# Two hybrid blocks on one core: building the state space operands a group later and into the down projection, with the modulation steps shifted the same way

## The chip, the core and the metric

The kernel runs on one core of a Trainium2 chip. Time is device microseconds of one execution of the whole program, from inputs in HBM to the output in HBM. The engines are TensorE (PE in the profile; PEld is its weight load), VectorE (DVE), ScalarE (ACT), GpSimd (POOL) and SyncE (SP), whose queue issues the DMAs. Each engine works through its own queue in order.

## What is computed

256 tokens of width 1024 go through a first block of two layers (a gated delta rule beside a short convolution, then a SwiGLU network) and a second block of two layers. The part that the change touches, cut to its core:

```python
def swiglu(h, w_in, w_out):                       # w_in 1024 x 5632, w_out 2816 x 1024
    gate, up = jnp.split(h @ w_in, 2, axis=-1)
    return (jax.nn.silu(gate) * up) @ w_out

def second_block(x, c, mod_w, mod_b, ...):
    for l in range(DEPTH):                        # DEPTH = 2
        mod = (jax.nn.silu(c) @ mod_w[l] + mod_b[l]).reshape(bsz, 3, 3, D_MODEL)
        ...
        x = post_add(x, swiglu(pre(x, 0), ffn_w_in[l, 0], ffn_w_out[l, 0]), 0, FFN_RES)
        y = token_mixer(pre(x, 1), ..., ssm_a_re[l], ssm_a_im[l], ssm_log_dt[l], ssm_b_re[l], ...)
        x = post_add(x, y, 1, 1.0)
        x = post_add(x, swiglu(pre(x, 2), ffn_w_in[l, 1], ffn_w_out[l, 1]), 2, FFN_RES)
    return x
```

Inside the token mixer `s5_ssm` runs a diagonal complex state space over the tokens. Its operands, products of B and C with powers of the decay, depend on weights alone. The modulation `mod` depends on the vector `c` alone. Both can be computed at any time before they are needed, beside other work.

## The kernel before

**Matmuls.** Every large product runs in float32 by three matmuls: weights and activations are split into a high part (`wh`, `xh`, `ah`) and a rest (`wl`, `xl`, `al`), and `group` (L270 on) adds wh·xh, wh·xl and wl·xh into PSUM. A matmul has a 128x128 stationary tile of weights and 256 tokens moving. Weights come as a stream of 586 blocks of up to eight tiles (512 KB), in the order in which they are used. `prepare` (L231) loads one block through SP, makes `wh` on ScalarE (L246; in the first block often on VectorE, L244) and `wl` on VectorE (L253, a "split" below). It runs four blocks ahead; there are four buffers of raw weights and four of `wl`. One block of eight tiles is 24 matmuls.

**The networks.** `ffn` (L429) goes over 22 tiles of the hidden width in six groups of four tiles (the last has two): `gp`, the gate product (4 blocks), Silu on ScalarE (L444), `up`, the up product (4 blocks), then on VectorE the product of the two (L459) and its split into `ah` and `al` (L387, L388). The PSUM banks (`pg`, four) that the next group's gate needs come free by that product. The first group differs, since the norm of its input isn't known yet: its input is settled behind it (L147 to L154), and its products take more operations (L446, L463, L464). Then comes the down projection, eight columns of 22 tiles (24 blocks); `done` takes each column on (its square is summed on VectorE at L601). The second block has four such networks, two a layer, with weights `f2i` (gate and up) and `f2o` (down).

**Work that rides along.** A modulation step (`mod_step`, L514) loads 512 KB through SP into `mraw`, a single buffer (`MB = 1`), and multiplies and sums it on VectorE (L521). There are 144. `mod_pace` (L524) adds a rate per weight block, `MOD_RATE`, by the kind of block (`phase_of`: 0 and 1 the first block's mixer and network, 2 the second block's mixer, 3 its networks), and issues a step at each full one. The state space operands of a layer are built by `ssm_params` (L1131), a generator in 27 steps: first 512-wide products on VectorE (L1143, L1161), then transposes and copies (L1191 on TensorE, L1192 on ScalarE), then 256 small matmuls and their copies (L1204, L1210), last the tables of cosines and sines, 36 short operations on VectorE. `ssm_start` (L1120) begins it behind a group of the last network ahead of that mixer, so in the first network of the second block for its layer 0, and in the second network of that layer for layer 1. `ssm_steps(rest)` (L1125) does as many steps as an even share over `rest` further calls needs.

**The order.** All this is only the order in which the program is written. `Order` (L1647 on) then plans the whole program with prices and priorities of its own and fixes for each engine the order in which its instructions are queued; data dependences and buffers bind it. A change in one place can so move instructions in all others.

Of the kernel before, what the change touches and what calls it, by code (L numbers as in the profile page):

```python
# [17 lines left out]
KD = 8  # L18
NF = 22
# [7 lines left out]
DEPTH = 2  # L27
HI_SHARE = (0.55,0.05,0,0)
WARM = 5
MOD_RATE = (0.08,0.5,0.03,0.4)  # L30
MB = 1
FF = 2816
NSTREAM = 74973184
# [39 lines left out]
def tiles4(o):  # L73
    return [o + c * P for c in range(4)]


def all_blocks():
# [14 lines left out]
    for l in range(DEPTH):  # L92
        w, o = ("win", l), 4 * DN_WIDTH + 8
        g(w, tiles4(512), KD)
        for c in (0, 1024, 1536, o + 512, o + 1024, o):
            g(w, tiles4(c), KD)
        for c in range(KD):
            g(("wout", l), [c * P], KD)
        ffn(("fg", l), ("fu", l), ("fd", l), 0)
# [58 lines left out]
class Kern:  # L158
# [270 lines left out]
    def ffn(s, wg, wu, wd, h, done, wg0=0, wu0=0, last=False, then=None):  # L429
        nc, tc = s.nc, s.tc  # L430
        rho = h.rho
        with tc.tile_pool(name=s.nm("ffn"), bufs=1, reuse_waits="tile") as pool:
            ah = s.t(pool, [P, NF, T], "ah", F32R)
            al = s.t(pool, [P, NF, T], "al", F32R)
            for g0 in range(0, NF, 4):
                n = min(4, NF - g0)
                gp = s.group(wg, [wg0 + (g0 + c) * P for c in range(n)], KD, h.h, h.l, fresh=h.due)
                due = h.behind(then)
                s.ssm_steps(2 * ((NF - 1 - g0) // 4) + 1)
                sg = []  # L440
                for c in range(n):
                    a = s.t(pool, [P, T], "sg", bufs=4)
                    if not due:
                        nc.scalar.activation(out=a, in_=gp[c][:, :T], func=AF.Silu)  # L444
                    else:
                        nc.vector.tensor_tensor(out=a, in0=gp[c][:, :T], in1=rho, op=ALU.mult)  # L446
                        bias = {}
                        if h.shift is not None:
                            cc = s.t(pool, [P, 1], "cc", bufs=4)
                            s.shifted(cc, gp[c])  # L450
                            bias = {"bias": cc}
                        nc.scalar.activation(out=a, in_=a, func=AF.Silu, **bias)
                    sg.append(a)
                up = s.group(wu, [wu0 + (g0 + c) * P for c in range(n)], KD, h.h, h.l, fresh=h.due)
                due = h.behind(then)
                for c in range(n):
                    a = s.t(pool, [P, T], "act", bufs=2)
                    if not due:
                        nc.vector.tensor_tensor(out=a, in0=up[c][:, :T], in1=sg[c], op=ALU.mult)  # L459
                    else:  # L460
                        cc = s.t(pool, [P, 1], "cc", bufs=4)
                        s.shifted(cc, up[c])
                        nc.vector.tensor_tensor(out=a, in0=up[c][:, :T], in1=rho, op=ALU.mult)  # L463
                        nc.vector.scalar_tensor_tensor(out=a, in0=a, scalar=cc, in1=sg[c], op0=ALU.add, op1=ALU.mult)  # L464
                    s.split(ah[:, g0 + c, :], al[:, g0 + c, :], a)
                if s.later and g0 == 0:
                    s.later(pool, ah[:, 0, 0:1])
                    s.later = None
                s.ssm_steps(2 * ((NF - 1 - g0) // 4))
            s.preload(AF.Sqrt, al[0:1, NF - 1, 0:1])  # L470
            AH, AL = (lambda k: ah[:, k, :]), (lambda k: al[:, k, :])
            if last:
                for half in range(2):
                    for c, ps in enumerate(s.group_by_token(wd, tiles4(half * 512), NF, AH, AL)):
                        done(half, c, ps)
            else:
                for c in range(KD):
                    done(c, s.group(wd, [c * P], NF, AH, AL)[0][:, :T])


    def open1(s, ctx):
# [4 lines left out]
    def layer1(s, l, x):  # L486
        nc = s.nc
        h = s.pre(x, s.cols(("g1", l)))
        x = s.mixer1(l, x, h)
        h = s.pre(x, s.cols(("g2", l)))  # L490
        if l == 0:
            s.later = s.first_coefs
        if l == DEPTH - 1:
            s.first_weights(h.rho[:, 0:KD])
        s.ffn(("fg", l), ("fu", l), ("fd", l), h,
              lambda c, ps: nc.vector.tensor_tensor(out=x[:, c, :], in0=x[:, c, :], in1=ps, op=ALU.add))
        return x
# [26 lines left out]
    def mod_pace(s, spec):  # L524

        if s.sc_ is None or not s.todo:
            return
        s.credit += MOD_RATE[s.phase_of(spec)]
        while s.credit >= 1 and s.todo:
            s.credit -= 1  # L530
            s.mod_step()
# [18 lines left out]
    def layer2(s, l, z, sq, last=False, subs=(0, 1, 2)):  # L550
        for i in subs:
            if i != 1 and (l if i == 0 else l + 1) == s.next_ssm < DEPTH:
                s.later = s.ssm_start
            s.mod_done(l, i)
            gains, weights = s.modA[l][:, i * 8:i * 8 + 8], None
            if sq is None:
# [1411 lines left out]
```

## Time and profile before

| | us |
|---|---|
| median of 3 runs | 1932.19 (1929.66 to 1932.62) |
| profiled execution | 1930.54 |
| its span, first to last instruction | 1928.7 |
| TensorE busy | 1868.8 |
| VectorE busy | 1525.5 |
| ScalarE busy | 1086.4 |
| mean granted TensorE clock | 0.987 of 2.4 GHz |

Matmuls are pipelined, and a matmul's row lasts longer than its share of the engine, so a busy TensorE may still be a slow one; how many matmuls a stretch holds, and how long it takes, tells more. In the second block the first layer's first network has its gate and up products from 700.5 to 853.5 us of the span and its down projection to 915.8; the second one from 1119.0 to 1271.4 and 1333.8; the second layer's from 1338.5 to 1467.5 and 1529.8, and from 1731.0 to 1859.4 and the end.

### The profile page before, as it was taken

The page shows a single profiled execution, that of the slowest core. Times are in us where ns is not written, and L with a number is a line of the kernel's source. Part 1 is how long each engine was busy: PE and PEld are TensorE (multiplying, and loading weights), DVE is VectorE, ACT ScalarE, POOL GpSimd, SP SyncE. Part 2 cuts the span into 40 slices and gives each one's busy share as a digit, 9 for nine tenths or more (in the row PEclk, how much of TensorE's full clock was granted, in tenths as well). Part 3 has the DMA queues.
Part 4 walks back from the last instruction along what each step waited for, and adds up shares of the span by engine and source line. Part 5 has one row for each costly group of instructions (what it writes and reads, how often), then busy time and mean ns, then how long its engine had stood idle before and what let it go on. Part 6 is the DMA issues. An engine that isn't in the chain of part 4 may idle for free.

```text
span 1928.7 us, 40170 instructions
## 1 busy us (share of the span) xinstructions
PE 1868.8 (97%) x16106; PEld 1812.7 (94%) x16106; DVE 1525.5 (79%) x2908; ACT 1086.4 (56%) x2004; POOL 8.5 (0%) x20
## 2 busy tenths in 40 slices
PE   7999999899899997999999999999999999999998
PEld 7999999899899997999898988999999988999997
DVE  8979877898887889886984799887977697479553
ACT  6767644576654564454755554556554565566442
POOL 0000000000000000000000000000000000000000
PEclk8999999999999998999999998999999999999999
DMA  5424787543577775577334546676777433455553
GB/s 196 144 99 155 283 279 267 206 139 115 207 274 276 265 268 197 208 267 258 110 122 146 203 164 231 223 266 212 258 280 252 161 135 123 141 173 172 189 187 109
DMA packets 107755, 383.78 MB, mean 199 GB/s; under 512 B 11952, under 2 KB 12464, under 8 KB 107568
## 3 DMA queue, kind: packets, MB, share of 16 engines
q1 hardware_dynamic: 107280, 380.83, 56.7%
q8 instruction: 126, 2.06, 0.4%
q14 instruction: 61, 0.50, 0.1%
q10 hardware_dynamic: 288, 0.39, 0.1%
HBM read 380.12 MB, written 1.05 MB: 198 GB/s over the span
## 4 chain that ended last, share of the span: by engine, by line
PE 82%; DVE 10%; ACT 5%; issue 2%; DMA 1%; SPq 0%; DVEq 0%; ACTq 0%
PE g L286 70%; PE g L306 3%; DVE wl L253 2%; DMA wr<-in_wstream 1%; ACT wh L246 1%; PE m L1204 1%; PE m L1242 1%; DVE xs L147 1%; DVE xl L405 1%; PE m L873 1%; DVE scp L1143 1%; DVE xl L154 1%; PE m L868 1%; DVE mraw L521 1%; DVE sqa L349 1%
## 5 line engine op out<-in xcount | busy, mean ns | idle before, releaser
L286 PE MATMUL g<-xh,wh 128*128 128x256 f32 (+1 forms) x3200 | 890.1, 287 | 23.9 <-DVE act L459 7.7
L286 PE MATMUL g<-xh,wl 128*128 128x256 f32 (+1 forms) x3200 | 886.5, 286 | 5.1 <-DVE wl L253 5.0
L253 DVE TENSOR_TENSOR wl<-wr,wh 128x1024 fp32r<-128x1024 f32 (+2 forms) x586 | 696.7, 1195 | 233.1 <-PE g L286 138.7
L286 PE MATMUL g<-xl,wh 128*128 128x256 f32 x3200 | 839.9, 285 | 0.7 <-DVE xl L405 0.4
L246 ACT CAST wh<-wr 128x1024 fp32r<-128x1024 f32 (+2 forms) x538 | 553.7, 1031 | 485.3 <-PE g L286 268.0
L286 PEld LDWEIGHTS g<-xh,wh 128*128 128x128 f32 x3200 | 605.6, 191 | 33.2 <-ACT wh L246 9.6
L286 PEld LDWEIGHTS g<-xh,wl 128*128 128x128 f32 x3200 | 606.1, 191 | 8.6 <-DVE wl L253 6.6
L286 PEld LDWEIGHTS g<-xl,wh 128*128 128x128 f32 x3200 | 580.7, 191 | 2.4 <-DVE xl L154 0.9
L286 PE MATMUL g<-ah,wl 128*128 128x256 f32 x880 | 246.4, 280 | 0.0
L286 PE MATMUL g<-ah,wh 128*128 128x256 f32 x880 | 245.5, 279 | 0.0
L286 PE MATMUL g<-al,wh 128*128 128x256 f32 x880 | 245.5, 279 | 0.0
L521 DVE SCALAR_TENSOR_TENSOR mraw<-mraw,siluc 128x1024 f32<-128x1024 f32 x144 | 175.5, 1219 | 27.4 <-DMA mraw<-in_modw 27.0
L286 PEld LDWEIGHTS g<-al,wh 128*128 128x128 f32 x880 | 165.4, 188 | 0.0
L286 PEld LDWEIGHTS g<-ah,wl 128*128 128x128 f32 x880 | 165.2, 188 | 0.0
L286 PEld LDWEIGHTS g<-ah,wh 128*128 128x128 f32 x880 | 164.6, 187 | 0.0
L387 ACT CAST ah<-act 128x256 fp32r<-128x256 f32 x132 | 50.5, 405 | 74.5 <-DVE act L459 62.5
L444 ACT ACTIVATE sg<-g 128x256 f32<-128x256 f32 x108 | 40.2, 385 | 43.1 <-PE g L286 43.0
L459 DVE TENSOR_TENSOR act<-g,sg 128x256 f32<-128x256 f32 x116 | 46.3, 418 | 15.3 <-PE g L286 13.0
L388 DVE TENSOR_TENSOR al<-act,ah 128x256 fp32r<-128x256 f32 x132 | 52.2, 417 | 6.0 <-ACT ah L387 4.1
L286 PE MATMUL g<-gl,wh 128*128 128x256 f32 x128 | 36.0, 281 | 0.0
L286 PE MATMUL g<-v,wl 128*128 128x256 f32 x128 | 35.9, 281 | 0.0
L286 PE MATMUL g<-v,wh 128*128 128x256 f32 x128 | 35.8, 280 | 0.0
(467 smaller groups left out, 2189.8 us busy)
## 6 DMA issues: line engine op xcount, KB each, us to landing
wr<-in_wstream SPq DMA_DIRECT2D x538, 512.0 KB, 4.3
mraw<-in_modw SPq DMA_DIRECT2D x144, 512.0 KB, 3.9
wr<-in_wstream SPq DMA_DIRECT2D x40, 384.0 KB, 4.7
wr<-in_wstream SPq DMA_DIRECT2D x8, 256.0 KB, 5.2
stb<-in_ssmc SPq DMA_DIRECT2D x2, 512.0 KB, 3.1
sbb<-in_ssmb SPq DMA_DIRECT2D x2, 512.0 KB, 3.4
x<-in_x SPq DMA_DIRECT2D x2, 256.0 KB, 5.5
x<-in_x SPq DMA_DIRECT2D x1, 512.0 KB, 7.7
```

The source lines that it names most:

```text
L147: nc.vector.scalar_tensor_tensor(out=a, in0=s.z[:, k, :], scalar=s.gains[:, k:k + 1], in1=s.rho, op0=ALU.mult, op1=ALU.mult)
L154: nc.vector.scalar_tensor_tensor(out=s.xl[:, k, :], in0=a, scalar=s.shift[:, k:k + 1], in1=s.xh[:, k, :T], op0=ALU.add, op1=ALU.subtract)
L246: nc.scalar.copy(out=hi[:, :n], in_=raw[:, :n])
L253: e.tensor_tensor(out=lo[:, :n], in0=raw[:, :n], in1=hi[:, :n], op=ALU.subtract)
L286: nc.tensor.matmul(ps[c][:, :x.shape[-1]], wt, x, start=bi == 0 and k == 0 and i == 0, stop=bi == len(specs) - 1 and k == n - 1 and i == ( ...
L306: nc.tensor.matmul(ps[h], x(k0 + k)[:, h * P:(h + 1) * P], wt[:, k, :], start=(k0 == 0 and k == 0 and i == 0), stop=(k0 + k == kt - 1 and ...
L349: nc.vector.tensor_tensor(out=acc, in0=acc, in1=q, op=ALU.add)
L387: s.nc.scalar.copy(out=out_h, in_=src)
L388: s.nc.vector.tensor_tensor(out=out_l, in0=src, in1=out_h, op=ALU.subtract)
L444: nc.scalar.activation(out=a, in_=gp[c][:, :T], func=AF.Silu)
L459: nc.vector.tensor_tensor(out=a, in0=up[c][:, :T], in1=sg[c], op=ALU.mult)
L521: nc.vector.scalar_tensor_tensor(out=w, in0=w, scalar=1.0, in1=s.sc_, op0=ALU.mult, op1=ALU.mult, accum_out=s.mod[l][:, j:j + 1])
```

## The change

The rate of modulation steps in the second block's gate and up products falls from 0.4 to 0.3 a weight block, and in its down projections it rises to 0.6. The state space steps start behind the group at 4, the second, and no longer behind the first. Their share counts KD = 8 further calls, which are made behind each column of the down projection. `later_at` tells the two users of `later` apart: the coefficients of the first block's network still start behind the first group.

```diff
-MOD_RATE = (0.08,0.5,0.03,0.4)
+MOD_RATE = (0.08,0.5,0.03,0.3,0.6)
...
-                s.ssm_steps(2 * ((NF - 1 - g0) // 4) + 1)
+                s.ssm_steps(2 * ((NF - 1 - g0) // 4) + 1 + KD)
...
-                if s.later and g0 == 0:
+                if s.later and g0 == s.later_at:
                     s.later(pool, ah[:, 0, 0:1])
                     s.later = None
-                s.ssm_steps(2 * ((NF - 1 - g0) // 4))
+                s.ssm_steps(2 * ((NF - 1 - g0) // 4) + KD)
...
                 for c in range(KD):
                     done(c, s.group(wd, [c * P], NF, AH, AL)[0][:, :T])
+                    s.ssm_steps(KD - 1 - c)
...
-            s.later = s.first_coefs
+            s.later, s.later_at = s.first_coefs, 0
...
-        s.credit += MOD_RATE[s.phase_of(spec)]
+        s.credit += MOD_RATE[4 if spec[0][0] == "f2o" else s.phase_of(spec)]
...
-                s.later = s.ssm_start
+                s.later, s.later_at = s.ssm_start, 4
```

What the planner makes of it, at three places of the first network of the second block. First VectorE's queue ahead of the second group's products (L459). `wl` rows are splits of weights, `mraw` a modulation step, `scp`, `smi` and `stb` the state space operands, `act` the product, `r` and `x` work of the network's entry. Before:

```order
L1143 TENSOR_TENSOR scp_9613<-scp_9613,smi_9612 128x16x32
L253 TENSOR_TENSOR wl_9785<-wr_9783,wh_9784 128x1024
L1143 TENSOR_TENSOR smi_9612<-scp_9613,ssm_lam 128x512
L1143 TENSOR_TENSOR scp_9613<-scp_9613,ssm_lam 128x16x32
L1143 TENSOR_TENSOR scp_9613<-scp_9613,smi_9612 128x16x32
L253 TENSOR_TENSOR wl_9815<-wr_9813,wh_9814 128x1024
L1143 TENSOR_TENSOR smi_9612<-scp_9613,ssm_lam 128x512
L521 SCALAR_TENSOR_TENSOR mraw_9819,mod_2605<-mraw_9819,siluc 128x1024
L1143 TENSOR_TENSOR scp_9613<-scp_9613,smi_9612 128x16x32
L253 TENSOR_TENSOR wl_9848<-wr_9846,wh_9847 128x1024
L253 TENSOR_TENSOR wl_9878<-wr_9876,wh_9877 128x1024
L459 TENSOR_TENSOR act_9906<-g_9779,sg_9771 128x256
```

And now (lines behind L479 are one further on in the new file, so L522 is the modulation step and L1144 the state space operations):

```order
L632 RECIPROCAL r_9251<-sd_9219 128x256
L253 TENSOR_TENSOR wl_9750<-wr_9748,wh_9749 128x1024
L522 SCALAR_TENSOR_TENSOR mraw_9784,mod_2605<-mraw_9784,siluc 128x1024
L253 TENSOR_TENSOR wl_9780<-wr_9778,wh_9779 128x1024
L640 TENSOR_TENSOR x_76<-x_76,r_9251 128x256 x2
L1144 TENSOR_TENSOR scp_9888<-stb_9889,ssm_cr 128x16x32
L1144 TENSOR_TENSOR smi_9887<-stb_9889,ssm_ci 128x512
L459 TENSOR_TENSOR act_9871<-g_9744,sg_9736 128x256
```

Between the fourth split for the second group's gate and that product there were 21 state space operations, 3 modulation steps and 8 splits; now 2 of the first stand there. From this product to the next group's there are now 15 of them, with 8 splits and 2 modulation steps.

Second, TensorE's small matmuls of the build (`m` from `scp` and `sbb`). Before they stand among gate and up products (`xh`, `xl`):

```order
L286 MATMUL g_10567<-xh_9172,wh_10492 128x256
L286 MATMUL g_10567<-xl_9173,wh_10492 128x256
L286 MATMUL g_10567<-xh_9172,wl_10493 128x256
L1204 MATMUL m_10694<-scp_9613,sbb_9615 32x32
L1204 MATMUL m_10694<-scp_9613,sbb_9615 32x128
L1204 MATMUL m_10694<-scp_9613,sbb_9615 32x96
L1204 MATMUL m_10694<-scp_9613,sbb_9615 32x64
```

Now they stand among the matmuls of the down projection (`ah`, `al`):

```order
L1205 MATMUL m_11074<-scp_9888,sbb_9890 32x128
L1205 MATMUL m_11074<-scp_9888,sbb_9890 32x96
L1205 MATMUL m_11074<-scp_9888,sbb_9890 32x64
L1205 MATMUL m_11074<-scp_9888,sbb_9890 32x32
L286 MATMUL g_11111<-ah_9271,wh_10899 128x256
L286 MATMUL g_11111<-al_9272,wh_10899 128x256
L286 MATMUL g_11111<-ah_9271,wl_10900 128x256
```

All of the build's transposes and matmuls have moved so, but for eight at either edge.

Third, VectorE's queue inside the first of these down projections (`sqa` sums the squares of the columns). Before:

```order
L253 TENSOR_TENSOR wl_11335<-wr_11333,wh_11334 128x1024
L601 TENSOR_TENSOR sqa_11266<-sqa_11266,sqb_11357 128x256
L521 SCALAR_TENSOR_TENSOR mraw_11398,mod_2606<-mraw_11398,siluc 128x1024
L253 TENSOR_TENSOR wl_11364<-wr_11362,wh_11363 128x1024
L253 TENSOR_TENSOR wl_11394<-wr_11392,wh_11393 128x768
L521 SCALAR_TENSOR_TENSOR mraw_11460,mod_2606<-mraw_11460,siluc 128x1024
L253 TENSOR_TENSOR wl_11427<-wr_11425,wh_11426 128x1024
```

Now:

```order
L522 SCALAR_TENSOR_TENSOR mraw_11379,mod_2606<-mraw_11379,siluc 128x1024
L253 TENSOR_TENSOR wl_11375<-wr_11373,wh_11374 128x1024
L253 TENSOR_TENSOR wl_11408<-wr_11406,wh_11407 128x768
L522 SCALAR_TENSOR_TENSOR mraw_11412,mod_2606<-mraw_11412,siluc 128x1024
L602 TENSOR_TENSOR sqa_11056<-sqa_11056,sqb_11463 128x256
L253 TENSOR_TENSOR wl_11441<-wr_11439,wh_11440 128x1024
L1144 TENSOR_TENSOR sbb_9890<-stb_9889,ssm_pw 128x512
L1144 TENSOR_TENSOR stb_9889<-stb_9889,sbb_9890 128x16x32
L1144 TENSOR_TENSOR stb_9889<-stb_9889,ssm_pw 128x16x32
L522 SCALAR_TENSOR_TENSOR mraw_11511,mod_2606<-mraw_11511,siluc 128x1024
```

The tables' operations (`ssm_pw`) and more modulation steps now stand between the splits: 13 steps in the 24 blocks of each of the first two of these down projections, and in the third 9 in its first 16 blocks, 8 of these within 13.

## Rows read from the trace of the kernel before

**Rows 1.** The page's first part: busy time, share, instructions of each engine.
```profile
PE 1868.8 (97%) x16106; PEld 1812.7 (94%) x16106; DVE 1525.5 (79%) x2908; ACT 1086.4 (56%) x2004; POOL 8.5 (0%) x20
```

**Rows 2.** Busy time by stretch (start:end, length, engines, clock): gate/up, four networks.
```profile
core 0: us, PE busy (x) PEld busy (x) DVE busy (x) ACT busy (x) POOL busy (x), PEclk, DMA share, GB/s
700.50:853.50 153.00, 142.26 (x1339) 139.72 (x1338) 140.75 (x259) 81.07 (x134) 3.13 (x5) 0.97 0.64 227
1119.00:1271.40 152.40, 146.03 (x1338) 142.50 (x1339) 142.23 (x267) 78.37 (x129) 3.12 (x5) 0.96 0.59 209
1338.50:1467.50 129.00, 128.24 (x1067) 127.26 (x1068) 107.71 (x183) 72.25 (x116) 0.00 (x0) 1.00 0.71 243
1731.00:1859.40 128.40, 128.27 (x1076) 128.03 (x1077) 90.74 (x155) 71.67 (x114) 0.00 (x0) 1.00 0.51 175
```

**Rows 3.** The same view of four down projections, the first of the first block.
```profile
638.40:700.50 62.10, 62.10 (x530) 62.10 (x529) 48.50 (x71) 30.33 (x41) 0.00 (x0) 1.00 0.74 268
853.50:915.80 62.30, 62.30 (x531) 62.30 (x530) 40.72 (x53) 30.37 (x42) 0.00 (x0) 1.00 0.77 258
1271.40:1333.80 62.40, 62.40 (x531) 62.40 (x530) 42.87 (x60) 30.43 (x42) 0.00 (x0) 1.00 0.77 262
1467.50:1529.80 62.30, 62.30 (x531) 62.30 (x530) 35.89 (x46) 30.04 (x41) 0.00 (x0) 1.00 0.65 224
```

**Rows 4.** The same view of the stretches with stalls, and those right behind.
```profile
739.00:773.50 34.50, 25.84 (x195) 25.46 (x194) 34.06 (x53) 14.04 (x20) 0.00 (x0) 0.85 0.56 202
1159.80:1191.50 31.70, 28.12 (x195) 26.82 (x194) 31.70 (x50) 14.71 (x22) 0.00 (x0) 0.84 0.59 212
755.00:765.20 10.20, 5.75 (x27) 5.78 (x28) 10.20 (x20) 4.60 (x7) 0.00 (x0) 0.50 0.46 161
773.50:796.20 22.70, 22.70 (x194) 22.70 (x193) 21.95 (x34) 11.01 (x16) 0.00 (x0) 1.00 0.67 248
1191.50:1214.20 22.70, 22.70 (x194) 22.70 (x193) 22.46 (x34) 8.72 (x15) 0.00 (x0) 1.00 0.60 221
```

**Rows 5.** TensorE in order of time: start, length, instruction, count, wait and releaser.
```profile
759.45 0.55 PE L286 MATMUL g<-xh,wh 128*128 128x256 f32 x1 [7.70 <-DVE act L459]
...
760.23 0.41 PE L286 MATMUL g<-xh,wh 128*128 128x256 f32 x1
760.44 0.41 PE L286 MATMUL g<-xl,wh 128*128 128x256 f32 x1
```

**Rows 6.** VectorE in order of time in the same stall.
```profile
740.88 1.22 DVE L521 SCALAR_TENSOR_TENSOR mraw<-mraw,siluc 128x1024 f32<-128x1024 f32 x1
...
742.03 0.68 DVE L1143 TENSOR_TENSOR smi<-scp,ssm_lam 128x512 f32<-128x512 f32 x1
742.63 1.21 DVE L253 TENSOR_TENSOR wl<-wr,wh 128x1024 fp32r<-128x1024 f32 x1
743.77 0.68 DVE L1143 TENSOR_TENSOR scp<-scp,smi 128x512 f32<-128x512 f32 x1
...
758.89 0.75 DVE L459 TENSOR_TENSOR act<-g,sg 128x256 f32<-128x256 f32 x2
759.56 0.68 DVE L1143 TENSOR_TENSOR scp<-scp,ssm_lam 128x512 f32<-128x512 f32 x1
```

**Rows 7.** Busy time by stretch again: the two that hold the build's matmuls.
```profile
796.30:841.90 45.60, 45.60 (x562) 44.29 (x560) 36.44 (x76) 25.89 (x43) 3.13 (x5) 1.00 0.63 220
1214.30:1259.90 45.60, 45.38 (x563) 44.13 (x561) 37.56 (x77) 25.78 (x43) 3.12 (x5) 1.00 0.69 241
```

**Rows 8.** Steps of 638.4 to 700.5 and 1271.4 to 1333.8: SP's wait, groups, landings.
```profile
SPq L520 <- DVE mraw L521: 39.8, 10, 5.0
...
mraw<-in_modw SPq DMA_DIRECT2D x11, 512.0 KB, 3.5
...
L521 DVE SCALAR_TENSOR_TENSOR mraw<-mraw,siluc 128x1024 f32<-128x1024 f32 x10 | 12.2, 1224 | 10.4 <-DMA mraw<-in_modw 10.4
...
mraw<-in_modw SPq DMA_DIRECT2D x10, 512.0 KB, 4.8
```

**Rows 9.** Busy time by stretch: entries of the first block's networks, layer 1, layer 0.
```profile
510.40:529.90 19.50, 14.18 (x100) 13.62 (x99) 17.20 (x34) 11.05 (x22) 0.00 (x0) 0.82 0.61 209
164.60:176.70 12.10, 11.82 (x101) 11.65 (x99) 11.98 (x24) 8.03 (x15) 0.00 (x0) 1.00 0.67 219
```

## The prediction

> **What bounds the kernel now.** I read the page's first part, then busy times by stretch, then the order of time inside the stretches that are longer than their twins. TensorE is busy 97% of the span and VectorE 79% [rows 1], so the end is set by TensorE, and the question is where TensorE runs below its pace. The pace is read in a down projection, which is nothing but 528 matmuls (8 columns x 22 tiles x 3 parts): 62.3 us [rows 3], 118 ns each. A gate/up part of these networks is 1056 matmuls, so 124.7 us at that pace. The four networks of the second block have the same code and the same sizes; two of them also build a layer's state space operands. The two without take 129.0 and 128.4 us for gate/up, the two with take 153.0 and 152.4 [rows 2]. So 24.0 us over the twin in each, 48.0 in all, and VectorE is busy 140.8 and 142.2 us there against 107.7 and 90.7 in the twins [rows 2].
>
> The 24.0 us have two parts. In a later stretch of each, 45.6 us long, three groups of 96 matmuls (34.0 us at 118 ns) run beside the 240 matmuls and 32 transposes that build the operands; TensorE is busy without a gap [rows 7]. 45.6 - 34.0 = 11.6 us is real TensorE work. The other 12.4 us are stalls. They sit mostly in two stretches: 34.5 and 31.7 us for 192 matmuls each that need 22.7, so 11.8 and 9.0 over; VectorE is busy in 34.06 and 31.70 of them [rows 4]. In the first, TensorE waits 7.70 us for the product of gate and up (L459) [rows 5]: VectorE has gone through state space operations and modulation steps that stand ahead of it in its queue, without a pause [rows 6]. Then comes a second price: for 10.2 us the granted clock is 0.50, the lower of the two levels, 1.2 GHz [rows 4], and a matmul takes 0.21 us instead of 0.118 [rows 5]. TensorE had just stood still when the clock fell.
>
> **The change, part by part.** *Start a group later.* In the order of before, 8 weight splits, 3 modulation steps, 21 state space operations and the tail of the network's entry (17 operations of 256: input settled, first products) stand between the fourth split for the second group's gate and that group's products. By the starts in [rows 6] a split takes 1.14 us, a step 1.15, a 512-wide operation 0.60 and a 256-wide one 0.34: 9.1 + 3.5 + 12.6 + 5.7 = 31 us, against 8 blocks x 24 matmuls x 0.118 = 22.7 us of TensorE. That lump is the stall. In the changed order only 2 state space operations stand ahead of the first products. The entry's surplus work then has the group to itself.
>
> *Spread into the down projection.* From the second group on, between the first products of one group and those of the next, the new order has 15 state space operations, 8 splits, 2 modulation steps and 8 operations of 256: 9.0 + 9.1 + 2.3 + 2.7 = 23.1 us against 22.7. So VectorE is still full, 0.4 us over in each of three such stretches, but no longer by 9. The 36 short operations of the tables move behind the last product, and so do all matmuls of the build: they cost TensorE the same 11.6 us there, since in a down projection it has no gap to hide them in [rows 3]. So 0 gained or lost on those, and the down projections become 62.3 + 11.6 = 74 us. VectorE has room: 40.7 and 42.9 us busy of 62 [rows 3], plus some 10 of tables and 4 of steps, is 55 of 74. ScalarE's copies of the build (L1192, L1210) move along beside 30 us busy [rows 3] and stay hidden. The two loads of the operands' inputs move one group later in SP's queue; the first operation that needs them moves as far. GpSimd's fills go with their step, and nothing else is in its queue.
>
> *Modulation steps.* 0.3 a block instead of 0.4 in gate/up, 0.6 in the down projection: 14 + 14 steps in the first network's program instead of 18 + 10, none added or removed in all. Each taken out of a full gate/up part relieves VectorE by 1.15 us, which the sum above contains. Added to a down projection each costs another transfer through the one buffer: its load waits in SP's queue for the step before, weight loads wait behind it, and splits wait behind the step on VectorE. In the new order the first down projection holds 13 steps, one in 74 / 13 = 5.7 us. What can be had: in the first block's down projection 11 steps ran in 62.1 us, one in 5.65, with SP 39.8 us waiting for that buffer, and TensorE lost nothing [rows 3, 8]. In the later one 10 steps waited 10.4 us for landings, which took 4.8 us instead of 3.5 [rows 8]; 4.8 + 1.22 + 0.1 = 6.1 us a cycle. 13 x 6.1 is 79, against 74 plus a lead of four weight buffers, 4 x 2.6 = 10.4 us. So from nothing to a few us; I take 1.5 for each of three down projections. The bounds are 0 and 9 (a cycle of 7.2: 13 x 7.2 - 84.4).
>
> Here a rule speaks against the change. The Trainium skill, "Trainium Kernel Development and Optimization", Best Practices, says to double-buffer so that transfers overlap with compute; this moves more steps through a single buffer into the stretch with the busiest queues. "DMA: Bandwidth & Descriptors", Anatomy of one DMA, fits a transfer at 2.0 us plus bytes / 436 GB/s, an estimate of 3.2 us for 512 KB; with it the cycle would be 4.5 us and the loss nothing. The trace has 3.5 and 4.8 as medians, and these decide.
>
> **The sum.** 48.0 us over the twins, less 23.2 of build matmuls that stay, is 24.8. About 0.8 stays at the first network's entry, which also applies the first block's last norm. 24.0. Less 2.5 for a VectorE that is still full (0.4 x 3 by the count in each network; bounds 0 and 5 each), less 4.5 for the steps' buffer: 17 us. The profiled execution took 1930.5 us (1928.7 of span), so 1913.5; the median of the runs is 1932.2, which gives 1915. I say 1914.
>
> **The rivals.**
> *VectorE stays the bound.* For it: 23.1 against 22.7 us leaves nothing for its own waits, and in the first network outside the 45.6 us of the build it stood still for (153.0 - 45.6) - (140.8 - 36.4) = 3.0 of 107.4 us [rows 2, 7]. Then each network loses 4 to 5 us, and a stall of that size may drop the clock again: 10.2 us at half speed are 5 us. 6 to 7 us a network gives 24 - 13 = 11 less the steps' 1.5 to 4.5: 1922 to 1926. Against it: right behind the two lumps VectorE was busy for 21.95 and 22.46 of 22.7 us, and TensorE did its 192 matmuls in just that time [rows 4].
>
> *The planner's shuffle.* The order is planned for the whole program, and the new one differs in the first block too, which the edit doesn't touch. How much that is worth: entering the second network of layer 1's block, 19.5 us went by at a clock of 0.82 for some 100 matmuls, where the first layer's entry took 12.1 at 1.00 [rows 9]. So one such entry is worth 7 us, either way: 1903 to 1907 if it is healed, 1922 if another one breaks. Two go wrong: 1929, about no change.
>
> *Slower: the single buffer decides.* If the steps' cycle in the down projections is 7.3 us rather than 5.7 to 6.1, VectorE stands in front of an unlanded load with the splits behind it: 13 x 7.3 - 84.4 = 10.5 us in each of the two, and in the third network's, with 8 steps in 13 blocks (34 + 10.4 us for 7 cycles), 7. Sum 28, against a gain of 21.5 without the steps' term: 1937 to 1941. It turns at a cycle of 7.0 us. Against it: the slowest of the stretches read, the one with the landings of 4.8 us, comes to 6.1 [rows 8]. It is the rule on double-buffering of the Trainium skill's Best Practices, named above, taken to its end; the trace bears it out only in the 10.4 us of waits.
>
> That the change doesn't do what it says is excluded by the order below.
>
> **How the numbers follow.** Forecast (1908 to 1921) 0.60; VectorE stays the bound (1921 to 1927) 0.17; a shuffle that heals an entry (1902 to 1908) 0.09; a shuffle that eats it up (1928.4 to 1936) 0.08; slower 0.06. About 0.2%, 3.9 us, is what a measurement of this kernel can tell from no change. Faster is 0.60 + 0.17 + 0.09 = 0.86, same 0.08, slower 0.06. The range 1904 to 1927 leaves out the last two cases and a part of the third.
>
> **What would show it.** Right: gate/up parts of 131 to 134 us in all four networks, down projections of 74 to 77 us in the two that build operands, no TensorE wait for L459 over 2 us, no half clock inside those networks, steps in the down projections 5.5 to 6.3 us apart. Wrong: gate/up still at 138 or more with VectorE busy throughout (the first rival); down projections over 80 us with VectorE waiting for the steps' loads (the third); or the first 700 us of the span longer or shorter by over 4 us (the second).

## The result, and the profile after

| | before, us | after, us |
|---|---|---|
| median (4 runs each) | 1932.4 (1929.66 to 1935.4) | 1906.55 (1904.44 to 1909.5) |
| profiled execution | 1930.54 | 1904.44 |
| its span | 1928.7 | 1902.7 |

The ratio is 0.9867, with an interval of 0.9846 to 0.9888: faster by 25.9 us, where 18 were forecast. The forecast of 1914 is 7.5 us too slow; the measured time lies near the fast end of the range of 1904 to 1927.

The first line of the page answers to [rows 1]: TensorE is busy 11.6 us less, VectorE nearly as long as before.

```profile
PE 1857.2 (98%) x16106; PEld 1802.4 (95%) x16106; DVE 1521.7 (80%) x2908; ACT 1088.3 (57%) x2005; POOL 8.3 (0%) x20
```

Next the busy times by stretch, as in [rows 2, 3] (start:end, length, busy time and instructions of each engine, clock, DMA): gate/up and down projection of the first network, of the second and of the third, which builds nothing, and the gate/up of the fourth.

```profile
core 0: us, PE busy (x) PEld busy (x) DVE busy (x) ACT busy (x) POOL busy (x), PEclk, DMA share, GB/s
697.30:826.50 129.20, 129.11 (x1086) 128.76 (x1085) 127.27 (x214) 78.07 (x123) 0.00 (x0) 1.00 0.74 250
826.50:896.70 70.20, 70.20 (x784) 68.18 (x783) 52.59 (x97) 34.78 (x55) 3.12 (x5) 1.00 0.69 248
1101.30:1231.30 130.00, 128.19 (x1067) 127.29 (x1068) 127.98 (x226) 70.79 (x113) 0.00 (x0) 1.00 0.68 230
1231.30:1304.60 73.30, 73.30 (x802) 71.16 (x801) 55.62 (x103) 35.88 (x56) 3.12 (x5) 1.00 0.68 240
1311.10:1439.60 128.50, 127.27 (x1066) 126.85 (x1067) 103.37 (x176) 72.56 (x117) 0.00 (x0) 1.00 0.65 234
1439.60:1502.00 62.40, 62.40 (x531) 62.38 (x530) 39.71 (x52) 30.33 (x43) 0.00 (x0) 1.00 0.71 249
1704.60:1833.80 129.20, 128.45 (x1076) 128.03 (x1077) 89.76 (x155) 71.61 (x114) 0.00 (x0) 1.00 0.50 173
```

The two gate/up parts fell from 153.0 and 152.4 us to 129.2 and 130.0, level with the twins, and the clock is 1.00 in all of them. VectorE is busy in 127.3 of 129.2 us: it is still full, but no lump of it stands in front of TensorE. The two down projections grew from 62.3 and 62.4 us to 70.2 and 73.3. The same view of the three stretches behind the first products of the second group, 192 matmuls each, answers to [rows 4]:

```profile
742.70:765.50 22.80, 22.80 (x194) 22.80 (x193) 22.43 (x35) 12.45 (x18) 0.00 (x0) 1.00 0.68 247
765.50:788.30 22.80, 22.80 (x194) 22.80 (x193) 22.80 (x36) 11.02 (x16) 0.00 (x0) 1.00 0.71 238
788.30:811.10 22.80, 22.71 (x191) 22.50 (x190) 22.77 (x35) 11.19 (x16) 0.00 (x0) 1.00 0.72 249
```

They last 22.8 us, where 34.5 and 31.7 stood before. VectorE in order of time at the place of the old stall answers to [rows 6] (start, length, instruction, wait and releaser):

```profile
740.11 0.77 DVE L640 TENSOR_TENSOR x<-x,r 128x256 f32<-128x256 f32 x2
741.47 0.69 DVE L1144 TENSOR_TENSOR scp<-stb,ssm_cr 128x512 f32<-128x512 f32 x1 [0.59 <-DMA stb<-in_ssmc]
742.08 0.69 DVE L1144 TENSOR_TENSOR smi<-stb,ssm_ci 128x512 f32<-128x512 f32 x1
742.68 0.42 DVE L459 TENSOR_TENSOR act<-g,sg 128x256 f32<-128x256 f32 x1
```

Two operations of the build stand ahead of the product, as the order had it. The 0.59 us for the operands' load are new and cost nothing: TensorE has no wait at all in that network's gate/up, and 2.2 us of waits in the second's.

The two stalls of before were not alike. In the first network TensorE waited for L459 [rows 5]. In the second it had no wait for L459: it waited for splits (`wl`) that stood behind operations of the build in VectorE's queue, and then the clock was at half there too. The wait (us in total, times, longest) and the stretch, before:

```profile
PE g L286 <- DVE wl L253: 3.4, 3, 2.4
```

```profile
1174.80:1185.00 10.20, 9.09 (x40) 8.20 (x39) 10.20 (x19) 3.53 (x6) 0.00 (x0) 0.50 0.65 225
```

TensorE was busy for 5.75 us [rows 4] and 9.09 us of the two stretches at half clock. My estimate from these rows is that half of that, 7.4 us, of the 20.8 us that the two stalled stretches took too long was the price of the clock; the rest was mostly waiting.

Where the 26.0 us of span went, from the same marks in both traces: up to the first network's gate 3.2 us less; the two gate/up parts 23.8 and 22.4 less; the two down projections 7.9 and 10.9 more; between the two networks 1.4 more, behind the second network 1.8 more, and 1.4 more from the third network's gate to the end.

### The profile page after: what moved, and what is told of

Read it like the earlier page. It is cut to its first block, busy times and chain, and to the rows that moved or that the text cites. A ratio compares the mean times of both kernels' runs of the same rounds, so it can differ in the third digit from the quotient of the medians.

```text
span 1902.7 us, 40195 instructions
## 1 busy us (share of the span) xinstructions
PE 1857.2 (98%) x16106; PEld 1802.4 (95%) x16106; DVE 1521.7 (80%) x2908; ACT 1088.3 (57%) x2005; POOL 8.3 (0%) x20
## 4 chain that ended last, share of the span: by engine, by line
PE 81%; DVE 8%; ACT 5%; DMA 3%; issue 2%; SPq 0%; DVEq 0%; ACTq 0%
PE g L286 69%; PE g L306 3%; DVE wl L253 2%; DMA wr<-in_wstream 2%; ACT wh L246 1%; DMA mraw<-in_modw 1%; PE m L1205 1%; PE m L1243 1%; DVE mraw L522 1%; DVE sqa L349 1%; PE m L874 1%; DVE xl L405 1%; PE m L869 1%; PE m L1331 0%; ACT sq L742 0%
## 5 line engine op out<-in xcount | busy, mean ns | idle before, releaser
L522 DVE SCALAR_TENSOR_TENSOR mraw<-mraw,siluc 128x1024 f32<-128x1024 f32 x144 | 176.0, 1222 | 26.0 <-DMA mraw<-in_modw 25.3
L444 ACT ACTIVATE sg<-g 128x256 f32<-128x256 f32 x108 | 39.5, 384 | 31.7 <-PE g L286 31.4
L459 DVE TENSOR_TENSOR act<-g,sg 128x256 f32<-128x256 f32 x116 | 45.9, 421 | 7.0 <-PE g L286 5.5
```

Of the source, the lines that this page charges most:

```text
L522: nc.vector.scalar_tensor_tensor(out=w, in0=w, scalar=1.0, in1=s.sc_, op0=ALU.mult, op1=ALU.mult, accum_out=s.mod[l][:, j:j + 1])
```

## The experiments

The stage times below are read in each kernel's trace at the same marks: gate/up and down projection of the first network, then of the second. Before: 153.0, 62.3, 152.4, 62.4, in sum 430.1. After: 129.2, 70.2, 130.0, 73.3, in sum 402.7, so 27.4 less. Every median stands against runs of the kernel before on the same chip. My theory A is the prediction's: a lump of VectorE work stalls TensorE, and taking it apart is the gain. The rivals are the rates and the planner's shuffle.

**The build alone** (rates as before).

```diff
-MOD_RATE = (0.08,0.5,0.03,0.3,0.6)
+MOD_RATE = (0.08,0.5,0.03,0.4,0.4)
```

> The build starts later and is spread as in the changed kernel; the modulation rates stay at 0.4 and 0.4 a weight block. Theory A (the lump of state space operations on VectorE made the stalls, the rates add a little room): 4 steps of 1.15 us stay in each of the two gate/up parts, so VectorE, which is busy 10.8 to 11.4 us of each 11.4 us stretch there after the change, goes 2 to 4.6 us over in each; gate/up 131 to 134 us, the whole 1910 to 1917 us. Theory B (the rates carry about half of the gain): 1917 to 1924. Theory C (the planner's shuffle made the gain): no relation to the edit, and the first 700 us differ by over 4 us.

1907.1 us against 1930.6; ratio 0.9876 (0.9859 to 0.9892). That is the whole gain within what can be told. Stages 129.4, 72.3, 131.1, 73.1, in sum 24.2 less than before. The time is below theory A's range, but the kernel did not get the four more steps in each gate/up on which that range rests. The modulation steps of the two gate/up parts in the trace (length, VectorE's busy time in L522 and its instructions, two to a step), first of the changed kernel, then of this run:

```profile
697.30:826.50 129.20, 18.51 (x30) 1.00 0.74 250
1101.30:1231.30 130.00, 17.24 (x28) 1.00 0.68 230
```

```profile
698.50:827.90 129.40, 20.87 (x34) 1.00 0.72 252
1106.80:1237.90 131.10, 18.39 (x30) 1.00 0.64 223
```

So the planner moves steps by itself. It had 15 and 14 there with the new rates and 17 and 15 with the old ones, and the parts with these two steps and one more took 0.2 and 1.1 us longer. The run shows what setting the rates is worth, which is nothing that can be told; it does not show what four steps would cost. Theory B falls; C falls too, since the first 700 us are within 2 us of before (698.5) and the gain lies in the two networks.

**The rates alone.** The build starts behind the first group and must end with gate/up, as before (from the changed kernel):

```diff
-                s.ssm_steps(2 * ((NF - 1 - g0) // 4) + 1 + KD)
+                s.ssm_steps(2 * ((NF - 1 - g0) // 4) + 1)
...
-                s.ssm_steps(2 * ((NF - 1 - g0) // 4) + KD)
+                s.ssm_steps(2 * ((NF - 1 - g0) // 4))
...
-                    s.ssm_steps(KD - 1 - c)
...
-                s.later, s.later_at = s.ssm_start, 4
+                s.later, s.later_at = s.ssm_start, 0
```

> Only the modulation rates change, 0.3 in gate/up and 0.6 in the down projections; the build stands where it stood before. Theory A: of the lump of 31 us against 22.7 us of TensorE one or two steps of 1.15 us go; the stall on the product of gate and up falls from 7.7 to some 6 us, the half clock behind it stays; 1926 to 1932 us. Theory B: 1917 to 1924. A loss, if the single buffer of the steps holds the down projections up (62.3 us each before): 1933 to 1940.

1939.0 against 1930.6; ratio 1.004 (1.0025 to 1.0054): slower. Its stretches (gate/up and down projection of the first network, gate/up of the second and the third), and TensorE's longest wait in the first:

```profile
699.10:847.70 148.60, 141.06 (x1258) 137.98 (x1256) 136.06 (x244) 81.67 (x133) 3.12 (x5) 0.98 0.65 226
847.70:913.00 65.30, 65.30 (x611) 64.67 (x610) 47.07 (x68) 29.85 (x43) 0.00 (x0) 1.00 0.73 252
1118.00:1269.00 151.00, 142.78 (x1307) 139.23 (x1307) 138.97 (x261) 78.52 (x130) 3.11 (x5) 0.98 0.59 206
1338.40:1470.20 131.80, 128.94 (x1067) 127.44 (x1068) 105.28 (x177) 72.74 (x118) 0.00 (x0) 1.00 0.67 232
```

```profile
PE g L286 <- DVE act L459: 4.5, 1, 4.5
```

The stall remains: TensorE waits 4.5 us for L459 in the first network, where I expected some 6, and 4.5 us in the second. The longer down projection is no stall: TensorE ran 80 instructions more in it, the build's matmuls that the plan let slip over the edge, and the two networks together are 1.2 us shorter. The loss lies in small pieces elsewhere, 2.8 us of it in the third network's gate/up. The trace, taken from the fastest of its runs, shows only 4 of the 8 us. The time lies in the range that I had given to the single buffer holding the down projections up, but TensorE has no wait in either of them. What the 8 us are stays open.

**The later start alone, and the spread alone**, with the old rates. The first takes the three edits of `ssm_steps` above, the second the one of `later_at`.

> The build begins a group later but must end with the gate and up products, as before; rates 0.4 and 0.4. Theory A: the same work of VectorE in one group less, so the lump moves from the second group into the later ones: gate/up 143 to 152 us in the two networks, down projections 62.3 us, the whole 1918 to 1932. Rival (only the entry's pile mattered, a group later is enough): gate/up about 129 + 11.6 = 141 us in both, no wait of over 2 us, the whole 1905 to 1911.

> The build begins behind the first group as before, but is spread on through the down projection; rates 0.4 and 0.4. Theory A: two steps at a call instead of three, so some 8 of the 21 state space operations of 0.6 us that stand ahead of the second group's products move behind them: 31 - 5 = 26 us against 22.7, a stall of 2 to 4 us, perhaps with a stretch at half clock; gate/up 131 to 138 us, the whole 1910 to 1920. Rival (the later start is what counts): the stall stays at 6 us or more with its half clock in both networks, 1920 to 1928.

Later start: 1922.2 against 1930.6, ratio 0.9953 (0.9938 to 0.9968); stages 147.3, 62.4, 150.8, 62.3, 7.3 less. Spread: 1911.5, ratio 0.9900 (0.9885 to 0.9915); stages 135.7, 68.1, 139.3, 66.9, 20.1 less. The gate/up parts, first of the later start, then of the spread:

```profile
700.80:848.10 147.30, 140.10 (x1338) 138.42 (x1337) 136.60 (x248) 83.52 (x136) 3.12 (x5) 0.99 0.67 235
1114.10:1264.90 150.80, 144.84 (x1339) 142.26 (x1340) 132.86 (x228) 78.30 (x128) 3.12 (x5) 0.95 0.59 205
```

```profile
700.10:835.80 135.70, 132.69 (x1121) 131.21 (x1119) 129.99 (x217) 77.73 (x126) 3.13 (x5) 1.00 0.71 254
1108.30:1247.60 139.30, 135.71 (x1140) 133.73 (x1141) 130.89 (x228) 73.31 (x120) 3.13 (x5) 0.99 0.63 222
```

With the later start alone the lump only moves: TensorE still waits for L459, 4.4 us in two pieces. With the spread alone that wait is 1.3 us in the first network, less than the 2 to 4 that I expected. Both together, at these rates, gave 24.2 (the build alone, above); so the later start adds 4.1 us to the spread's 20.1, and the two overlap by 3.2. The spread is worth far more than the later start. My other expectations held, but for an upper end of the second gate/up with the spread that I had 1 us too low. The prediction had named the later start first, as what takes the lump away.

**More steps in the down projections**, for the third rival.

```diff
-MOD_RATE = (0.08,0.5,0.03,0.3,0.6)
+MOD_RATE = (0.08,0.5,0.03,0.2,0.8)
```

> The changed kernel with the rates 0.2 and 0.8 instead of 0.3 and 0.6: 18 steps in each down projection that has steps, against 12 or 13. Through one buffer a step takes 5.2 to 5.7 us there in the changed kernel's trace, so 18 take 94 to 103 us; the stretch is 70 to 73 us long, and a lead of four weight buffers is 10.4 us. If VectorE stands in front of a load that has not landed, with the weight splits behind it (the prediction's third rival), each of two down projections grows by 10 to 20 us: 1925 to 1945 us in all. If the steps only fall behind their rate, because the planned order lets the splits pass, nothing is lost in the down projections and the late steps pile up at the network's end: 1906 to 1914. If the room that they leave in gate/up were still worth something: 1902 to 1906.

1958.6 against 1929.5, ratio 1.0136 (1.0113 to 1.0160): 52 us slower than the changed kernel. The three down projections that have steps take 92.2, 93.8 and 76.7 us instead of 70.2, 73.3 and 62.4, while gate/up is 127.3 and 128.1, only 1.9 less each. That is beyond what I expected. The down projections by stretch, then ScalarE's longest wait, SP's, and the steps' loads in the first of them (waits: us in total, times, longest; loads: count, size, median us):

```profile
825.90:918.10 92.20, 81.18 (x821) 76.60 (x819) 59.98 (x108) 38.55 (x65) 3.04 (x5) 0.96 0.60 209
1251.90:1345.70 93.80, 85.42 (x820) 77.96 (x818) 58.38 (x110) 37.62 (x62) 3.13 (x5) 0.96 0.56 198
1481.50:1558.20 76.70, 68.30 (x531) 65.65 (x530) 43.48 (x58) 30.85 (x42) 0.00 (x0) 0.96 0.67 228
```

```profile
ACT wh L246 <- DMA wr<-in_wstream: 30.7, 10, 6.3
...
SPq L521 <- DVE mraw L522: 48.7, 11, 6.2
...
mraw<-in_modw SPq DMA_DIRECT2D x17, 512.0 KB, 3.6
```

17 steps in 92.2 us are one in 5.4. The steps' loads land about as fast as before, VectorE is idle a third of the time, and what comes late are the weights: ScalarE waits 30.7 us for them, and their loads stand in SP's queue behind the steps' loads, which wait 48.7 us in all for the one buffer. So the third rival's mechanism is real. It turned not on a slower cycle, as the prediction had it, but on how many steps fall on the weight blocks: 12 or 13 in a stretch fit in the changed kernel, 17 don't. In the third network 10, close together, already cost 14.3 us. The prediction's own sum falls short here: 17 x 5.4 = 92 us against 70.2 and a lead of 10.4 would be 11 us more, and 22 were measured. The Trainium skill ("Trainium Kernel Development and Optimization", Best Practices) says to double-buffer so that transfers overlap with compute. At this rate the trace agrees with it; up to a rate of 0.6 no wait of TensorE in a down projection bears it out. A second buffer was not tried.

**All steps in gate/up.**

```diff
-MOD_RATE = (0.08,0.5,0.03,0.3,0.6)
+MOD_RATE = (0.08,0.5,0.03,0.6,0)
```

> The changed kernel with the rates 0.6 and 0: all modulation steps of the second block's networks in gate and up, 26 in each instead of 13, none in the down projections. If VectorE is full in the stretches with the build's operations (it is busy 10.8 to 11.4 of each 11.4 us there after the change), 13 more steps of 1.15 us are up to 15 us more in each of the two gate/up parts; the groups without the build have some room, so 6 to 13 each: 1918 to 1933 us, with waits of TensorE for VectorE in them. If the rates don't matter (as 0.4 and 0.4 against 0.3 and 0.6 hardly did): 1905 to 1911.

1945.2 against 1929.5, ratio 1.0067 (1.0045 to 1.0090). Gate/up of the three networks, TensorE's longest waits in the first, and the stretch of the third at half clock:

```profile
697.00:847.80 150.80, 138.41 (x1097) 135.02 (x1096) 140.85 (x236) 79.65 (x127) 2.99 (x4) 0.97 0.71 254
1120.20:1268.10 147.90, 137.26 (x1096) 134.69 (x1097) 140.50 (x246) 72.97 (x119) 2.99 (x4) 0.97 0.67 240
1342.60:1480.70 138.10, 132.71 (x1066) 131.18 (x1067) 113.41 (x194) 70.97 (x118) 0.00 (x0) 0.96 0.70 241
```

```profile
PE g L286 <- DVE wl L253: 8.9, 7, 3.6
PE g L286 <- DVE act L459: 1.3, 2, 1.1
```

```profile
1356.20:1366.40 10.20, 9.07 (x41) 8.84 (x42) 7.91 (x20) 4.67 (x8) 0.00 (x0) 0.50 0.82 257
```

The whole is 12 us above the range that I had put. The trace has 26 and 24 steps in the first two gate/up parts instead of 15 and 14. VectorE's 13.6 us more in the first (127.3 to 140.9) became 21.6 us of TensorE, above the 6 to 13 I had put. So VectorE at 98% in the changed kernel stands near an edge: with two more steps and one more the parts took 0.2 and 1.1 us longer, with eleven and ten more 21.6 and 17.9. The third network, which builds nothing and has VectorE busy only 113.4 of 138.1 us, lost 9.6. That is not a full VectorE: about half of it is the half clock for 10.2 us near its entry, 4.5 us by TensorE's 9.07 us of work there. Together the last two runs bracket the rates: 0.3 and 0.6 take as long as 0.4 and 0.4, while 0.2 and 0.8 lose 52 us, in the down projections, and 0.6 and 0 lose 39, in gate/up.

**The pace of the down projections.** In the changed kernel's trace some stretches of the two grown down projections run faster than any before. TensorE alone by stretch (busy time and instructions, clock, DMA share, GB/s), one of 20 us in each of three down projections: before, then after.

```profile
870.00:890.00 20.00, 20.00 (x173) 1.00 0.75 256
1280.00:1300.00 20.00, 20.00 (x172) 1.00 0.82 284
1470.00:1490.00 20.00, 20.00 (x173) 1.00 0.75 263
```

```profile
870.00:890.00 20.00, 20.00 (x179) 1.00 0.66 239
1280.00:1300.00 20.00, 20.00 (x179) 1.00 0.74 266
1470.00:1490.00 20.00, 20.00 (x172) 1.00 0.73 270
```

From start to start a matmul takes 113.3 ns in the first two after, and 117.8 in all others. The two paces never mix within a row of like matmuls; they change only where something else interrupts the row or where the down projection begins. In the first down projection 457 of 528 matmuls have the faster one, in the second 334: 2.0 and 1.5 us. Five runs tried to find what sets it. First extra transposes in the kernel before (the build's code is untouched):

```diff
         specs = group_blocks(w, colstarts, kt, korder)
+        if kt == NF:
+            for _ in range(colstarts[0] // P % 4 + 1):
+                nc.tensor.transpose(ps[0][:, T:T + P], s.ident, s.ident)
```

> The kernel before with one to four extra 128x128 transposes ahead of each column of the five down projections that go by columns (40 breaks, 100 transposes, their results unused). In the changed kernel the dense matmuls of a down projection stand either 117.8 ns apart or 113.3 ns, and each stretch between two pieces of the build has one of the two. Theory P (a break in the row of like matmuls decides anew which of the two it is): some of the 40 columns of 66 matmuls run at 113.3; the breaks cost 100 x 0.109 + 40 x 0.09 = 14.5 us, and with half of the columns at 113.3 some 6 us come back: about 1939 us. Theory Q (the faster pace comes from something else that the build does beside it): all columns stay at 117.8, 1945 us.

1941.7 against 1929.5. All 40 columns ran at 117.8 ns: theory P fell. The whole is 12.2 us longer than before, where I had put 14.5 us for the breaks alone. Next 32 small matmuls ahead of four columns of each other down projection, and the changed kernel once more:

```diff
+        if kt == NF and not s.steps and colstarts[0] < 4 * P:
+            pb = s.pg.tile([P, 512], F32, tag="g", name=s.nm("g"))
+            for j in range(4):
+                for i in range(2):
+                    for t in range(SL):
+                        nc.tensor.matmul(pb[32 * t:32 * t + 32, j * P + 32 * t:(j + 1) * P], s.ident[:, 0:32],
+                                         s.ident[:, 0:P - 32 * t], start=i == 0, stop=i == 1, tile_position=(0, 32 * t))
```

> The changed kernel with 32 extra small matmuls, of the build's shapes and into a PSUM bank of their own, ahead of each of the first four columns of the three down projections that go by columns and have no build (12 breaks of some 0.9 us, results unused). The extra transposes of the run before left every column at 117.8 ns, so a break alone does not do it. Theory P2 (it takes small matmuls, or another PSUM bank, between the like ones): a part of the 12 columns, and of the 264 matmuls behind the fourth break, at 113.3; about 1906.5 + 10.6 - 1 to 6 = 1911 to 1916. Theory Q2 (it comes from something else in the two networks with the build): all at 117.8, 1917.

> The changed kernel once more, for a second trace. If the pace of 113.3 ns is fixed by the order of the instructions, the same stretches of the two down projections have it again (from 847.9 us to the end of the first, and 1255.2 to 1262.9 and 1274.4 to 1304.4 in the second); if it falls by chance at each execution, others do. The time 1904 to 1909 either way.

1920.9 us, 4 us above what I had put for theory Q2, and 117.8 ns behind all twelve breaks. The repeat took 1905.9 us (ratio 0.9869) and had the faster pace in the same stretches, matmul for matmul, so it is fixed by the program and not by chance. Then breaks of 1 to 24 small matmuls:

```diff
+            s.breaks = getattr(s, "breaks", 0) + 1
+            for n in range(s.breaks):
+                t = n % SL
+                nc.tensor.matmul(pb[32 * t:32 * t + 32, 32 * t:P], s.ident[:, 0:32],
+                                 s.ident[:, 0:P - 32 * t], start=True, stop=True, tile_position=(0, 32 * t))
```

> The changed kernel with a break of small matmuls (32 columns of weights, 128 to 32 moving columns, into a bank of their own, results unused) ahead of each column of the three down projections that go by columns and have no build; the first break has 1 matmul, the next 2, and so on to 24. The run before had twelve breaks of 32, all with 117.8 ns behind them, and two traces of the changed kernel had the 113.3 ns in the same stretches, so the order of instructions fixes the pace. If the number of small matmuls in a break decides, some of the 24 sizes give 113.3 ns for the 66 matmuls behind them and the others don't, and a size that does can be put at the head of each down projection. If it is something of the build's own, all 24 stay at 117.8. The breaks cost 300 x 0.03 + 24 x 0.2 = 14 us, so about 1920.

1926.0 us in a single execution. The plan tore the last two breaks apart, so 22 sizes were tried: behind 11 and 12 the row ran at 113.3 ns, behind the 20 others at 117.8. Four columns of 66 matmuls, behind breaks of 10, 11, 12 and 13:

```profile
649.00:656.80 7.80, 7.80 (x67) 7.78 (x66) 5.55 (x7) 4.12 (x7) 0.00 (x0) 1.00 0.70 261
657.70:665.30 7.60, 7.60 (x67) 7.54 (x66) 5.71 (x9) 3.00 (x5) 0.00 (x0) 1.00 0.70 233
666.20:673.70 7.50, 7.50 (x67) 7.50 (x66) 5.97 (x8) 2.56 (x4) 0.00 (x0) 1.00 0.84 284
674.90:682.70 7.80, 7.80 (x66) 7.76 (x66) 5.28 (x7) 4.70 (x6) 0.00 (x0) 1.00 0.69 231
```

So 11 and 12 were tried where they should pay, in place of the growing break:

```diff
+        at, size = {("fd", 0): (0, 11), ("fd", 1): (1, 11), ("f2o", 1, 0): (0, 12)}.get(w, (-1, 0))
+        if kt == NF and colstarts[0] == at * P:
+            pb = s.pg.tile([P, 512], F32, tag="g", name=s.nm("g"))
+            for n in range(size):
```

> The changed kernel with one break in each of the three down projections that go by columns and have no build: 11 small matmuls ahead of the first column in the first layer's, 11 ahead of the second column in the second layer's, 12 ahead of the first column in the third. In the run before, breaks of 11 and of 12 were the only ones of 24 sizes with 113.3 ns behind them. If the size alone decides, 528 + 462 + 528 matmuls gain 4.5 ns each, 6.8 us, less three breaks of 1.0: 1906 - 4 = 1902 us. If what stands ahead of the break counts too (there matmuls of the same down projection, here gate and up products in two of three), the second alone gains and the whole is within 2 us of the changed kernel. If neither, 1909.

1906.2 us, ratio 0.9875 (0.9859 to 0.9892): no difference from the changed kernel, and all three rows stayed at 117.8 ns. Two rows of 66 matmuls in the networks with the build, which the edit does not touch, even fell from 113.3 ns in the changed kernel to 117.8. The size of the break does not decide by itself. What does stays open.

## Why the prediction was right, and where its sizes were off

The direction and the mechanism held: TensorE set the end, a lump of the build's work on VectorE made the stalls, and taking it apart removed the waits and the half clock behind them. The two halves run alone show the gain where the prediction placed it, in these two networks. The prediction read the wait of the first network only; in the second the same lump stood in front of splits and not of L459. The size was less well forecast: 25.9 us instead of 18. The time lies among the 1902 to 1908 that the prediction gave, with a chance of 0.09, to a shuffle that heals an entry, and that is not what brought it there: the first part of the span gave 3.2 us, and other places lost 4.6. The terms for the down projections were too dear, and 3.5 us of the gain, the faster pace of the matmuls there, were luck. By its own list:

- *Gate/up 131 to 134 us in all four:* 129.2, 130.0, 128.5 and 129.2, below it. The terms for the entry, 0.8 us, and for a VectorE still full, 2.5, measured 1.8 together: the two parts lie 0.2 and 1.6 us over their twins of before. In the first this even holds 20 of the build's 32 transposes, 2.2 us at 109 ns each, which the trace has ahead of the down projection. VectorE was indeed busy throughout (22.4 to 22.8 of 22.8 us), but with this order in its queue that cost TensorE next to nothing. The first rival's 6 to 7 us a network did not come; the run with all steps in gate/up lost 18 to 22 us a network with ten and eleven more steps.
- *Down projections 74 to 77 us:* 70.2 and 73.3. This is the step with the largest miss. The build's matmuls were put at the same 23.2 us in both places and the steps' buffer at 4.5, together 27.7 us; measured are 18.8. Of the 8.9 us between, 3.5 are the faster pace, which nothing in the trace before had shown; it has 117.8 ns in every down projection. Another 2.2 are the transposes that stayed in the first gate/up. The other 3.2 come off the buffer's 4.5, of which 1.3 at most were paid: TensorE has no wait in any of the three down projections, and the third, with steps but without the build, is 62.4 us, as before.
- *Steps 5.5 to 6.3 us apart:* so it was, 5.7 us in the first and 5.9 in the second, as means from the first step's start to the last one's. The buffer's term took the landings of 4.8 us of one stretch as its slow case; the medians are 3.4 in the first and 3.7 in the second:

```profile
mraw<-in_modw SPq DMA_DIRECT2D x11, 512.0 KB, 3.4
...
mraw<-in_modw SPq DMA_DIRECT2D x12, 512.0 KB, 3.7
```

- *No TensorE wait for L459 over 2 us, no half clock inside the networks:* so it was. In the second network the first of these signs could not tell, since no wait for L459 stood there before.
- *The planner's shuffle:* the first 700 us are 3.2 shorter, and three places behind the networks 1.4, 1.8 and 1.4 us longer: 1.4 us lost in sum. Over eight kernels, before and after among them, the first part took 697.0 to 700.8 us. So a shuffle is worth 1 to 4 us a place here, where the rival had 7.
- *The rates:* the sum counted each step taken out of gate/up as 1.15 us of relief. Undoing the rates cost nothing that the medians show, though the planner put only two steps and one back, and the rates alone made the kernel slower. So this relief was not needed: the build's change alone freed enough.

Together: 1.5 us for VectorE and the entry (3.3 less 1.8) and 8.9 in the down projections were better than the 17 us of the sum, and 1.4 elsewhere worse: 17 + 1.5 + 8.9 - 1.4 = 26.0, the difference of the spans.

## What to carry to other kernels

An engine off the critical path may be busy 98% of a stretch and cost the bounding engine next to nothing, if what that engine waits for stands early in its queue; look for lumps ahead of such an operation, not at the share alone. Read each stall's own wait: the two here ended on different instructions of the same queue. Work that rides along is best spread over every stretch that has room, and how much one buffer can carry in a stretch is the number of transfers times their cycle (here 5.3 to 5.9 us), which turns sharply: 12 and 13 in 70 and 73 us were free, 17 cost 20 to 22 us. Take a change apart before crediting its parts, and count in the trace what each setting really moved: here the rates added nothing that can be told, and the planner had moved few steps for them.

## What the hardware showed unexpectedly

In the down projections rows of identical matmuls, 128x128 against 256 moving columns, ran at one of two paces at the same granted clock of 1.00: 117.8 ns, or 113.3 ns, which is 272 cycles of 2.4 GHz. The pace changes at an interruption or at the passage into the down projection, and nowhere else. Two traces of the same program agree on it, so the program fixes it and not chance, but neither 40 breaks of transposes nor twelve of 32 small matmuls brought it about, and breaks of 11 and 12 did in one place and not in others. The cause stays open. If it could be had in all down projections, each would gain 528 x 4.5 ns = 2.4 us. The Trainium skill ("TensorE: Matmul & The Clock Gate", Back-to-back issue gap) gives 262 cycles for 256 columns as the gap of an isolated matmul, and says that in a stream of weight loads and matmuls both set the spacing. Both paces of the stream here are above that gap, 272 and 283 cycles, and the section tells of no second one.
